# First norm of the first half: rows normalised by ScalarE, weight and bias per channel after the transpose, residual rows weighted when read back

## The chip, the core and the metric

The kernel runs on one core of a Trainium2 chip. The metric is the time of the program on the device, in microseconds (us); a row of the profile gives durations in us, means of groups in nanoseconds (ns). The core has five engines that run their own instruction queues in order: PE (TensorE, matmuls and transposes), DVE (VectorE), ACT (ScalarE), POOL (GpSimd) and SP (SyncE, which here only issues DMAs). They wait for each other by semaphores.

## The reference

One layer over 1024 positions of 1024 channels, in float32:

```python
def layer_norm(x, g, b):
    mu = jnp.mean(xf, axis=-1, keepdims=True)
    var = jnp.mean(jnp.square(xf - mu), axis=-1, keepdims=True)
    return (xf - mu) * lax.rsqrt(var + LN_EPS) * g + b
...
h = layer_norm(x, ln_in_g, ln_in_b)
u_glu, z, xbc, dt_raw, gate_a, gate_b = split_in(h @ w_in)
y_a = conformer_branch(u_glu, ...)
y_b = ssd_branch(z, xbc, dt_raw, ...)
mix = (sigmoid(gate_a) * y_a + sigmoid(gate_b) * y_b) @ w_o
h = layer_norm(DN_ALPHA * h + mix, ln1_g, ln1_b)
h = layer_norm(DN_ALPHA * h + conv_ffn(h, ...), ln2_g, ln2_b)
```

The normalised rows h are used twice: as input of the matmul with w_in, and as residual in the second norm.

## The kernel before

The 1024 positions are worked in two halves of 512, each of four tiles of 128 rows. For a half, `ln_in` loads the four x tiles, normalises them row by row on DVE, writes them to a scratch in DRAM (`h_scr`), and transposes them on PE into `hT`, which holds channels on the partitions. Then `mixers` does the two branches, `combine` gates and mixes them, and `out_proj` multiplies with w_o, adds the residual rows, which it reads back from `h_scr`, and normalises again. The order of the program is ln_in(0), mixers(0), combine(0), ln_in(1), out_proj(0), mixers(1), combine(1), and then the feed-forward part over all rows.

Precision is kept by splitting each float32 operand into a high part (a rounding cast, on ACT) and a low part (the difference, on DVE); each product is then three matmuls (L166, L167, L168). `weights` (L149) does this for a weight tile: DMA into `st_...` (L152), cast on ACT (L154), difference (L155), which is DVE's unless an engine is passed. `transpose_to` (L187) does it for four transposed blocks of 128x128 that fill one bank of PSUM: transposes on PE (L192), cast by ACT (L198), difference by DVE (L199).

The norm of a row tile is `ln_stats` (statistics L207 and L221 on DVE, square root L222 on ACT, reciprocal L223 on DVE) and `ln_apply`: two passes of DVE over 128x1024, (x - mean) * weight (L227) and times the reciprocal deviation plus bias (L230). Weight and bias are rows broadcast to all 128 partitions (`in_g`, `in_b`; `row`, L203).

`first_columns` (L348) starts on the first three column tiles of w_in before all rows are there: 144 matmuls of 128x256 (L357), where the left half (q = 0) needs the first two row tiles. For the first half (hh = 0) the low parts of these three weight tiles are made by POOL.

`out_proj` (L665) works in two column halves q of 512. For each it has four banks of PSUM, one for each row tile, and 96 matmuls; then DVE adds alpha times the residual row to each bank (L687). There are four banks of this kind, so PE begins q = 1 in a bank when L687 of q = 0 has read it.

Instructions are ordered by the tile framework: each engine's queue is fixed when the program is built, by readiness in the framework's own accounting and by priority (`tc.high_priority`). At run time each engine takes its queue in that order.

## Time and profile before

| quantity | value |
|---|---|
| median of 3 runs | 2032.83 us (2030.95 to 2035.71) |
| profiled execution, its own time | 2035.35 us |
| its span, first to last instruction | 2033.6 us |
| mean granted clock of TensorE | 0.991 |
| DMA over the span | 273.51 MB, 134 GB/s |

The time of an execution is a little longer than the span, which runs from the first to the last instruction that the profiler recorded. A row of the timeline gives the start, the duration, the engine, the line of the kernel file, the operation, its output and inputs, and in brackets how long its engine idled before and for whom. In a row of grouped instructions, the numbers behind the count are busy time in us, mean ns of one, and idle time before with its releasers.

### The profile page before, as it was taken

The page shows a single profiled execution, that of the slowest core. Times are in us where ns is not written, and L with a number is a line of the kernel's source. Part 1 is how long each engine was busy: PE and PEld are TensorE (multiplying, and loading weights), DVE is VectorE, ACT ScalarE, POOL GpSimd, SP SyncE. Part 2 cuts the span into 40 slices and gives each one's busy share as a digit, 9 for nine tenths or more (in the row PEclk, how much of TensorE's full clock was granted, in tenths as well). Part 3 has the DMA queues.
Part 4 walks back from the last instruction along what each step waited for, and adds up shares of the span by engine and source line. Part 5 has one row for each costly group of instructions (what it writes and reads, how often), then busy time and mean ns, then how long its engine had stood idle before and what let it go on. Part 6 is the DMA issues. An engine that isn't in the chain of part 4 may idle for free.

```text
span 2033.6 us, 24571 instructions
## 1 busy us (share of the span) xinstructions
PE 1978.0 (97%) x9164; PEld 1628.0 (80%) x9164; DVE 1710.7 (84%) x2285; ACT 1001.8 (49%) x1448; POOL 171.9 (8%) x141
## 2 busy tenths in 40 slices
PE   6999999999999999999999999998899999989998
PEld 6888887888788888888888888887778888777886
DVE  7599999989766869999998976596998788777868
ACT  4465654556453356665454645364334445443432
POOL 2010101001400000100100130010000000010000
PEclk9999999999999999999999999999999999999999
DMA  6212233332546522222423354565342232377563
GB/s 219 93 63 94 79 102 106 99 104 101 174 133 216 195 88 77 88 85 75 127 86 107 109 166 138 188 234 202 130 153 106 99 109 99 109 258 264 175 224 109
DMA packets 97303, 273.51 MB, mean 134 GB/s; under 512 B 11168, under 2 KB 11168, under 8 KB 97184
## 3 DMA queue, kind: packets, MB, share of 16 engines
q1 hardware_dynamic: 87696, 242.06, 35.9%
q0 software_dynamic: 7184, 25.69, 3.3%
q10 hardware_dynamic: 2304, 4.20, 0.6%
q8 instruction: 72, 1.18, 0.2%
q14 instruction: 47, 0.39, 0.1%
HBM read 222.36 MB, written 49.55 MB: 134 GB/s over the span
## 4 chain that ended last, share of the span: by engine, by line
PE 66%; DVE 24%; DMA 4%; issue 4%; ACT 1%; SPq 0%; DVEq 0%; ACTq 0%
PE acc L166 17%; PE acc L168 17%; PE acc L167 17%; DVE c L420 8%; PE sm L166 3%; PE sm L167 3%; PE sm L168 3%; DVE xbc L375 2%; DMA dr<-b_scr 1%; PE acc L357 1%; PE sm L534 1%; DVE fo L895 1%; DMA st_wo<-wo 1%; PE sm L515 1%; DVE w_so L155 1%
## 5 line engine op out<-in xcount | busy, mean ns | idle before, releaser
L420 DVE SCALAR_TENSOR_TENSOR c<-v,pc,c 128x512 f32<-128x512 f32 x480 | 375.3, 805 | 7.6 <-ACT c L409 6.1
L478 POOL TENSOR_TENSOR au<-seg_mv,head_of 128x1024 fp32r<-128x1024 f32 x32 | 76.3, 2383 | 962.2 <-PE sm L487 730.4
L166 PE MATMUL acc<-hT,w_c 128*128 128x512 f32 x352 | 141.1, 401 | 0.0
L167 PE MATMUL acc<-hT,w_c 128*128 128x512 f32 x352 | 140.7, 400 | 0.0
L168 PE MATMUL acc<-hT,w_c 128*128 128x512 f32 x352 | 138.5, 393 | 0.0
L895 DVE SCALAR_TENSOR_TENSOR fo<-u,pc,fo 128x1024 f32<-128x1024 f32 x88 | 111.5, 1279 | 8.5 <-ACT fo L891 7.8
L375 DVE SCALAR_TENSOR_TENSOR xbc<-u,pc,xbc 128x512 f32<-128x512 f32 x144 | 109.7, 774 | 0.7 <-ACT xbc L373 0.5
L167 PE MATMUL acc<-w_z,hT 128*128 128x512 f32 x256 | 100.9, 394 | 0.0
L166 PE MATMUL acc<-w_z,hT 128*128 128x512 f32 x256 | 100.9, 401 | 0.0
L168 PE MATMUL acc<-w_z,hT 128*128 128x512 f32 x256 | 100.7, 396 | 0.0
L1021 ACT CAST w_dn<-dr 128x1024 fp32r<-128x1024 f32 (+1 forms) x73 | 60.8, 842 | 77.7 <-DVE dr L951 31.5
L154 ACT CAST w_c<-st_c 128x1024 fp32r<-128x1024 f32 x50 | 52.5, 1051 | 86.8 <-PE acc L168 66.1
L1022 DVE TENSOR_TENSOR w_dn<-dr,w_dn 128x1024 fp32r<-128x1024 f32 (+1 forms) x73 | 69.6, 963 | 17.6 <-ACT w_dn L1021 17.5
L167 PEld LDWEIGHTS acc<-hT,w_c 128*128 128x128 f32 x352 | 66.2, 188 | 16.8 <-issue 3.8
L168 PEld LDWEIGHTS acc<-hT,w_c 128*128 128x128 f32 x352 | 66.1, 188 | 16.0 <-issue 2.6
L166 PEld LDWEIGHTS acc<-hT,w_c 128*128 128x128 f32 x352 | 66.1, 188 | 15.9 <-issue 2.6
L155 DVE TENSOR_TENSOR w_c<-st_c,w_c 128x1024 fp32r<-128x1024 f32 x47 | 60.6, 1289 | 20.2 <-ACT w_c L154 20.2
L166 PE MATMUL acc<-h1s,w_s 128*128 128x512 f32 x168 | 66.6, 397 | 5.7 <-ACT u L875 5.7
L166 PE MATMUL acc<-h1b,w_ue 128*128 128x512 f32 x176 | 68.9, 392 | 2.6 <-ACT w_ue L740 1.4
L166 PE MATMUL sm<-h1b,w_s 128*128 128x512 f32 x176 | 70.3, 400 | 0.0
L167 PE MATMUL sm<-h1b,w_s 128*128 128x512 f32 x176 | 70.3, 399 | 0.0
L168 PE MATMUL sm<-h1b,w_s 128*128 128x512 f32 x176 | 69.9, 397 | 0.0
(352 smaller groups left out, 5811.1 us busy)
## 6 DMA issues: line engine op xcount, KB each, us to landing
st_c<-wcol SPq DMA_DIRECT2D x50, 512.0 KB, 3.5
st_z<-wz SPq DMA_DIRECT2D x32, 512.0 KB, 3.4
st_wo<-wo SPq DMA_DIRECT2D x24, 512.0 KB, 3.8
ra<-wup SPq DMA_DIRECT2D x22, 512.0 KB, 3.6
rb<-wup SPq DMA_DIRECT2D x22, 512.0 KB, 3.4
t_scr<-fo POOLq DMA_DIRECT2D x22, 512.0 KB, 4.2
dr<-t_scr SPq DMA_DIRECT2D x44, 256.0 KB, 3.4
dr<-wdown SPq DMA_DIRECT2D x38, 256.0 KB, 3.8
```

The source lines that it names most:

```text
L154: A.copy(w[:, 0, :], st)
L155: (eng or V).tensor_tensor(out=w[:, 1, :], in0=st, in1=w[:, 0, :].bitcast(F32), op=ALU.subtract)
L166: TE.matmul(ps, wa(0), xa(0), start=start, stop=False, skip_group_check=more)
L167: TE.matmul(ps, wa(0), xa(1), start=False, stop=False, skip_group_check=more)
L168: TE.matmul(ps, wa(1), xa(0), start=False, stop=stop, skip_group_check=more)
L357: TE.matmul(ps[:, ts], w[:, i, k * P : (k + 1) * P], hT[:, j, k, ts], start=n == 0 and k == 0, stop=n == 2 and k == KD - 1,)
L375: V.scalar_tensor_tensor(out=o, in0=u[:, k : k + HALF], scalar=pc[:, wc + k : wc + k + 1], in1=o, op0=ALU.mult, op1=ALU.add,)
L420: V.scalar_tensor_tensor(out=accs[i], in0=v[:, k : k + HALF], scalar=pc[:, wc + k : wc + k + 1], in1=accs[i], op0=ALU.mult, op1=ALU.add,)
L478: G.tensor_tensor(out=au, in0=seg_mv[:, c, :].unsqueeze(1).to_broadcast([P, 8, P]), in1=head_of[:, g, :].unsqueeze(2).to_broadcast([P, 8, P]),
L895: V.scalar_tensor_tensor(out=o, in0=u[:, k : k + T], scalar=pc[:, wc + k : wc + k + 1], in1=o, op0=ALU.mult, op1=ALU.add,)
L1021: A.copy(w[:, 0, cs], src)
L1022: V.tensor_tensor(out=w[:, 1, cs], in0=src, in1=w[:, 0, cs].bitcast(F32), op=ALU.subtract)
```

## The change

The first half gets a norm of its own, `ln_first`. The two affine steps of the norm are taken apart. (x - mean) / deviation is one activation on ACT per row tile, with the scale 1/deviation and a shift of -mean/deviation per row. Weight and bias of the norm come after the transpose, when channels are partitions and both are one number per partition (new columns of `pc`, the per-channel constants): ACT and DVE take turns in evicting 128x128 blocks from PSUM into a float32 tile `v`, from which the high part (ACT) and the low part (DVE) are made. The rows written to `h_scr` are without weight and bias; `out_proj` of the first half loads the two broadcast rows (`res_g`, `res_b`) and applies them on POOL to the rows read back. The four loads of x are preceded by a small load of the new constants, and PE does 40 transposes of the identity at the start. The low parts of the first three weight tiles are DVE's instead of POOL's. The second half's norm is as before.

```diff
@@ -39,7 +39,9 @@
-PC_N = PC_FB + 44
+PC_IG = PC_FB + 44
+PC_IB = PC_IG + 8
+PC_N = PC_IB + 8
...
@@ -231,31 +233,73 @@
+    def ln_first():
+
+        hT = big_tile("hT0")
+        with pool("lnin0", side="right") as pl:
+            with tc.high_priority(offset=8000):
+                SY.dma_start(pc[:, PC_IG:PC_N], pcol[:, PC_IG:PC_N])
+                xts = []
+                for t in range(4):
+                    xt = pl.tile([P, D], F32, name=f"x0_{t}")
+                    SY.dma_start(xt, x[t * P : (t + 1) * P, :])
+                    xts.append(xt)
+                for n in range(10):
+                    pt = bank(1)
+                    for i in range(4):
+                        TE.transpose(pt[:, i * P : (i + 1) * P], ident, ident)
+            SY.dma_start(pc[:, :PC_IG], pcol[:, :PC_IG])
+            SY.dma_start(a_log, prow[RW_AL : RW_AL + HEADS].partition_broadcast(P))
+            SY.dma_start(dskip, prow[RW_SD : RW_SD + HEADS].partition_broadcast(P))
+            for t, xt in enumerate(xts):
+                ts = slice(t * P, (t + 1) * P)
+                with tc.high_priority(offset=6000 - 1000 * (t // 2)):
+                    mv, rs = ln_stats(pl, [xt], f"in0_{t}")
+                    shift = pl.tile([P, 1], F32, tag="shift", bufs=2, name=f"shift{t}")
+                    V.tensor_scalar(
+                        out=shift, in0=mv[:, 0, 0:1], scalar1=rs[:, 0:1], scalar2=-1.0,
+                        op0=ALU.mult, op1=ALU.mult,
+                    )
+                    A.activation(out=xt, in_=xt, func=AF.Identity, scale=rs[:, 0:1], bias=shift)
+                    SY.dma_start(h_scr[0][ts, :], xt)
+                    for q in range(2):
+                        pt = bank(0)
+                        for i in range(4):
+                            c = (4 * q + i) * P
+                            TE.transpose(pt[:, i * P : (i + 1) * P], xt[:, c : c + P], ident)
+                        v = pl.tile([P, 4, P], F32, tag="v", bufs=3, name=f"v0_{t}_{q}")
+                        for i in range(4):
+                            k = 4 * q + i
+                            src = pt[:, i * P : (i + 1) * P]
+                            g, b = pc[:, PC_IG + k : PC_IG + k + 1], pc[:, PC_IB + k : PC_IB + k + 1]
+                            if i % 2:
+                                V.tensor_scalar(
+                                    out=v[:, i, :], in0=src, scalar1=g, scalar2=b,
+                                    op0=ALU.mult, op1=ALU.add,
+                                )
+                            else:
+                                A.activation(out=v[:, i, :], in_=src, func=AF.Identity, scale=g, bias=b)
+                        hi, lo = (hT[:, i, 4 * q : 4 * q + 4, ts] for i in range(2))
+                        A.copy(hi, v)
+                        V.tensor_tensor(out=lo, in0=v, in1=hi.bitcast(F32), op=ALU.subtract)
+        return hT
+
     def ln_in(hh):
         hT = big_tile(f"hT{hh}")
         with pool(f"lnin{hh}", side="right") as pl:
-            first = hh == 0
-            xts, gb = [], []
+            gb = [row(pl, RW_ING, D, "in_g"), row(pl, RW_INB, D, "in_b")]
+            xts = []
...
@@ -347,7 +391,7 @@
-        ws = [weights(wcol[ct], f"c{hh}_{ct}", eng=None if hh else G) for ct in cts]
+        ws = [weights(wcol[ct], f"c{hh}_{ct}") for ct in cts]
...
@@ -668,6 +712,10 @@
         for t in range(4):
             SY.dma_start(rs[t], h_scr[hh][t * P : (t + 1) * P, :])
+        ing, inb = row(pl, RW_ING, D, "res_g"), row(pl, RW_INB, D, "res_b")
+        for r in rs:
+            G.tensor_tensor(out=r, in0=r, in1=ing, op=ALU.mult)
+            G.tensor_tensor(out=r, in0=r, in1=inb, op=ALU.add)
         sts = [pl.tile([P, 2, 6], F32, name=f"st_o{hh}_{t}") for t in range(4)]
...
@@ -1100,7 +1148,7 @@
-    hT = ln_in(0)
+    hT = ln_first()
```

`out_proj` is called for the first half alone; the second half has `out_proj_pairs`, which is unchanged.

The change also moves instructions. In the file of the change, all lines behind `ln_first` have other numbers: L230 becomes L232, L199 becomes L201, L155 becomes L157, L687 becomes L735.

First, ACT's queue at the very start of the program. Before, it is square roots (L222), casts of transposed blocks (L198, of PSUM banks sm) and casts of the first column weights (L154, w_c):

```order
L198 CAST hT_184<-sm_214 128x4x128
L198 CAST hT_184<-sm_221 128x4x128
L154 CAST w_c_40_306<-st_c_40_304 128x1024
L198 CAST hT_184<-sm_239 128x4x128
L154 CAST w_c_32_311<-st_c_32_309 128x1024
L198 CAST hT_184<-sm_246 128x4x128
L222 ACTIVATE rs_in_2_254<-mv_in_2_253,eps 128x1
L154 CAST w_c_36_316<-st_c_36_314 128x1024
L222 ACTIVATE rs_in_3_279<-mv_in_3_278,eps 128x1
L198 CAST hT_184<-sm_264 128x4x128
```

Now, the normalising activations (L263), block evictions (L281, into v) and casts of v (L283) stand in it. The rows up to the cast of v_1_0 are what the first column matmuls need:

```order
L263 ACTIVATE x_0_189<-x_0_189,shift_258,rs_in_0_251 128x1024
L281 ACTIVATE v_0_0_267<-sm_262,pc 128x128
L156 CAST w_c_40_397<-st_c_40_395 128x1024
L263 ACTIVATE x_1_191<-x_1_191,shift_294,rs_in_1_287 128x1024
L224 ACTIVATE rs_in_2_323<-mv_in_2_322,eps 128x1
L281 ACTIVATE v_0_1_279<-sm_274,pc 128x128
L281 ACTIVATE v_0_0_267<-sm_262,pc 128x128
L156 CAST w_c_32_402<-st_c_32_400 128x1024
L224 ACTIVATE rs_in_3_359<-mv_in_3_358,eps 128x1
L156 CAST w_c_36_407<-st_c_36_405 128x1024
L281 ACTIVATE v_1_0_303<-sm_298,pc 128x128
L263 ACTIVATE x_2_193<-x_2_193,shift_330,rs_in_2_323 128x1024
```

The evictions of different banks alternate in the queue, and the weight casts stand between them; six more rows (the norm of x_3 among them) follow before the cast of v_1_0.

Second, DVE's queue around the residual addition of the first half, where ln_in(1) is under way. Before:

```order
L227 SCALAR_TENSOR_TENSOR x_3_5153<-x_3_5153,mv_in_3_5234,in_g 128x1024
L223 RECIPROCAL rs_in_2_5210<-rs_in_2_5210 128x1
L687 SCALAR_TENSOR_TENSOR r_0_5263<-r_0_5263,acc_5279 128x512
L687 SCALAR_TENSOR_TENSOR r_1_5264<-r_1_5264,acc_5280 128x512
L687 SCALAR_TENSOR_TENSOR r_2_5265<-r_2_5265,acc_5281 128x512
L199 TENSOR_TENSOR hT_5143<-sm_5170,hT_5143 128x4x128
L223 RECIPROCAL rs_in_3_5235<-rs_in_3_5235 128x1
L199 TENSOR_TENSOR hT_5143<-sm_5177,hT_5143 128x4x128
L687 SCALAR_TENSOR_TENSOR r_3_5266<-r_3_5266,acc_5282 128x512
L230 SCALAR_TENSOR_TENSOR x_2_5151<-x_2_5151,rs_in_2_5210,in_b 128x1024
```

Now, from the second pass over x_2 on:

```order
L232 SCALAR_TENSOR_TENSOR x_2_5246<-x_2_5246,rs_in_2_5301,in_b 128x1024
L201 TENSOR_TENSOR hT_5234<-sm_5261,hT_5234 128x4x128
L201 TENSOR_TENSOR hT_5234<-sm_5268,hT_5234 128x4x128
L201 TENSOR_TENSOR hT_5234<-sm_5286,hT_5234 128x4x128
L232 SCALAR_TENSOR_TENSOR x_3_5248<-x_3_5248,rs_in_3_5326,in_b 128x1024
L201 TENSOR_TENSOR hT_5234<-sm_5293,hT_5234 128x4x128
L201 TENSOR_TENSOR hT_5234<-sm_5311,hT_5234 128x4x128
L157 TENSOR_TENSOR w_wo_1_2_5574<-st_wo_1_2_5572,w_wo_1_2_5574 128x1024
L201 TENSOR_TENSOR hT_5234<-sm_5318,hT_5234 128x4x128
L201 TENSOR_TENSOR hT_5234<-sm_5336,hT_5234 128x4x128
L201 TENSOR_TENSOR hT_5234<-sm_5343,hT_5234 128x4x128
L735 SCALAR_TENSOR_TENSOR r_0_5354<-r_0_5354,acc_5382 128x512
```

The addition to r_0 (L687, now L735) stood ahead of the second pass over x_2 and x_3 and of the low parts of hT; it now stands behind all of them and behind the split of w_wo_1_2.

Third, the new rows of POOL, behind the last row of the first half's conv norm (r_0 to r_3 are the residual tiles of the first half):

```order
L682 TENSOR_TENSOR var_4876<-var_4876,csq_7_4904 128x512
L717 TENSOR_TENSOR r_0_5354<-r_0_5354,res_g 128x1024
L717 TENSOR_TENSOR r_1_5355<-r_1_5355,res_g 128x1024
L717 TENSOR_TENSOR r_2_5356<-r_2_5356,res_g 128x1024
L717 TENSOR_TENSOR r_3_5357<-r_3_5357,res_g 128x1024
L718 TENSOR_TENSOR r_0_5354<-r_0_5354,res_b 128x1024
L718 TENSOR_TENSOR r_1_5355<-r_1_5355,res_b 128x1024
```

Where POOL had nothing between the end of the first half's conv norm and the second half's scan, it has eight passes (the additions to r_2 and r_3 are not shown); all multiplications stand ahead of the additions. On SP the two loads of `res_g` and `res_b` stand behind the four row loads, `res_g` ahead of the load of w_wo_1_2 and `res_b` ahead of that of w_wo_1_3. On PE, all 16 transposes of x_2 and x_3 in ln_in(1) now stand ahead of the first matmul of q = 1; before, they stood among these matmuls.

More of the change, by code (lines that the diff above doesn't have):

```diff
@@ L244, in ln_in @@
                     xts.append(xt)
[L245 to L258 removed]
+            for t, xt in enumerate(xts):
+                mv, rs = ln_stats(pl, [xt], f"in{hh}_{t}")
+                ln_apply(xt, mv, rs, 0, *gb)
+                SY.dma_start(h_scr[hh][t * P : (t + 1) * P, :], xt)
+                transpose_to(hT, xt, t, 0, KD)
         return hT
@@ L1179, in _pack @@
             chan(a["ffn_dw_b"][0]).T,
+            chan(a["ln_in_g"]).T,
+            chan(a["ln_in_b"]).T,
         ],
```

13 lines of the change are left out of this document (removed).

## The prediction

> **What bounds the kernel now.** I read the page first (busy shares and the chain of work that ended last), then the waits of PE, then the timeline of the two places that the change touches.
>
> ```profile
> PE 1978.0 (97%) x9164; PEld 1628.0 (80%) x9164; DVE 1710.7 (84%) x2285; ACT 1001.8 (49%) x1448; POOL 171.9 (8%) x141
> PE 66%; DVE 24%; DMA 4%; issue 4%; ACT 1%; SPq 0%; DVEq 0%; ACTq 0%
> PE sm L192 <- DVE x L230: 15.4, 3, 12.7
> ```
>
> PE is busy 97% of the span, and the chain runs through PE for 66%. POOL is all but idle. The longest wait of PE in the whole trace is for the normalised rows of L230, 15.4 us in three pieces, 12.7 of it at the start, which is what this change rewrites. The rest of the kernel is a nearly gapless queue on PE, so a delay of PE early on goes through unless something later has slack. Two places matter: the first 40 us (first half's norm) and 647 to 689 us, where the rows are read back as residual.
>
> **Place one, the front.** Rows of the timeline and of two tiles (x count, then min/median/max ns):
>
> ```profile
> 4.33 1.29 DVE L207 BATCH_NORM_STATS2 st_in<-x 128x6 f32<-128x512 f32 x2 [1.73 <-DMA x<-x]
> 8.83 2.48 DVE L227 SCALAR_TENSOR_TENSOR x<-x,mv_in,in_g 128x1024 f32<-128x1024 f32 x2 [1.58 <-DMA in_g<-prow]
> 12.71 3.40 PE L192 MATMUL sm<-ident,x 128*128 128x128 f32 x16 [12.71 <-DVE x L230]
> 17.99 5.12 DVE L227 SCALAR_TENSOR_TENSOR x<-x,mv_in,in_g 128x1024 f32<-128x1024 f32 x2
> 26.59 1.06 PE L192 MATMUL sm<-ident,x 128*128 128x128 f32 x8 [1.60 <-DVE x L230]
> L155 POOL TENSOR_TENSOR w_c<-st_c,w_c x3: 2395/3363/3375, 16.3 to 22.0; 128x1024 fp32r<-128x1024 f32 x3
> 29.95 9.36 PE L357 MATMUL acc<-hT,w_c 128*128 128x256 f32 x74
> 39.61 0.50 PE L166 MATMUL acc<-hT,w_c 128*128 128x512 f32 x1
> 689.23 17.43 PE L357 MATMUL acc<-hT,w_c 128*128 128x256 f32 x144
> L891 ACT ACTIVATE fo<-u,pc 128x1024 f32<-128x1024 f32 x44 | 49.7, 1149 | 20.1 <-DVE fo L923 8.7 <-DMA t_scr<-fo 5.2 <-DMA b_scr<-fo 4.1
> L154 ACT CAST w_c<-st_c 128x1024 fp32r<-128x1024 f32 x50 | 52.5, 1051 | 86.8 <-PE acc L168 66.1 <-issue 8.6 <-PE acc L357 6.8
> L373 ACT ACTIVATE xbc<-acc,pc 128x512 f32<-128x512 f32 x48 | 33.1, 689 | 0.0
> L371 ACT COPY u<-acc 128x512 f32<-128x512 f32 x48 | 27.6, 575 | 0.0
> L511 ACT COPY bt<-sm 128x128 f32<-128x128 f32 x28 | 7.3, 262 | 27.1 <-DVE cbm L498 27.1
> L182 ACT CAST mixT<-mb 128x512 fp32r<-128x512 f32 x16 | 10.0, 623 | 5.7 <-DVE mb L661 5.7
> 708.28 0.56 ACT L371 COPY u<-acc 128x512 f32<-128x512 f32 x1
> 708.74 0.19 ACT L372 COPY u<-u_halo 128x3 f32<-128x3 f32 x1
> L222 ACT ACTIVATE rs_in<-mv_in,eps 128x1 f32<-128x1 f32 x8 | 2.4, 299 | 12.4 <-DVE mv_in L221 8.8 <-DVE x L230 3.6
> ```
>
> What goes: the wait for in_g (1.58 us), four DVE pairs of 1024-wide passes, and the three POOL splits, whose contention stretched two of those passes to 5.12 us. What comes: one more small load ahead of x (estimate half a microsecond, so x_0 at 4.8), 40 warm-up transposes on PE while it has nothing else, and a chain on ACT. DVE's statistics of x_0 and x_1 (1.29 each, with the aggregates and the reciprocal between) let the first normalising activation start at about 8.0. ACT works in order, and up to the cast that gives the first column matmuls their last 128 columns (v_1_0) it has: 4 norms at 1.15 (nearest row L891, same shape) = 4.60; 3 casts of w_c at 1.05 = 3.15; 3 casts into hT at 0.62 (L182) = 1.87; 7 block evictions; 2 square roots at 0.30 = 0.60. A 128x128 eviction with scale and bias does not occur; L373 against L371 says that scale and bias add 0.114 to a plain copy, L511 that a plain 128x128 copy takes 0.262, so 0.38 each (0.26 to 0.45) = 2.66. Sum 12.9. An ACT start can lie before the end of the one ahead (by 0.10 at 708.74); 0.07 for 18 of them is -1.3; the evictions alternate between ACT and DVE on one PSUM bank, for which I add 1.0: columns begin at 8.0 + 12.9 - 1.3 + 1.0 = 20.6. DVE's share (blocks, and now the three lo splits of w_c at about 1.2) runs beside it. Then 144 column matmuls: half 1 shows 17.43 for the same 144 without a gap; four transposes that stand among them add 0.5, handing over 0.4: first 512-wide matmul at 38.9, against 39.61, **-0.7**.
>
> The clock decides the sign. The 16 transposes at 12.71 took 0.213 each, the eight at 26.59 0.133, so PE starts slow. The warm-up ends near 8 us; then come 28 transposes in pieces between 11 and 20 with PE mostly idle. If PE is slow again at 20.6, its first microseconds cost 1.6 (bounds below), so **+0.9**. The row for that comes from the other place. The Trainium skill ("TensorE: Matmul & The Clock Gate", What's actually happening) says that the throttle is the default and returns after an idle window of about 3.4 us; the idle PE between 8 and 11 would by that rule undo the warm-up, which gives the same +0.9. I take +0.9; ends -1.3 (evictions at 0.32, PE fast) and +2.5 (transposes slow too, on ACT's path).
>
> **Place two, the residual.** Rows of the timeline, of SyncE's DMA queue and of PE around it, of L670, and two stretches (PE, PEld, DVE, ACT, POOL busy, granted clock, DMA share, GB/s):
>
> ```profile
> DMA to landing us min/median/max: 10.8/10.9/11.0
> L670 SPq DMA_DIRECT2D r<-h_scr x4: 319/323/327, 647.3 to 650.9; - x4
> 653.03 1.56 SPq L152 DMA_DIRECT2D st_wo<-wo  x2
> SPq L152 <- DMA in_g<-prow: 1.7, 1, 1.7
> 656.00:658.00 2.00, 2.00 (x11) 1.65 (x10) 2.00 (x3) 0.00 (x0) 0.00 (x0) 1.00 1.03 420
> 655.03 0.39 PE L166 MATMUL acc<-w_wo,mixT 128*128 128x512 f32 x1
> 655.71 0.39 PE L166 MATMUL acc<-w_wo,mixT 128*128 128x512 f32 x1
> 663.09 1.86 DVE L687 SCALAR_TENSOR_TENSOR r<-r,acc 128x512 f32<-128x512 f32 x3
> 663.90 0.47 PE L166 MATMUL acc<-w_wo,mixT 128*128 128x512 f32 x1 [0.85 <-DVE r L687]
> 667.58 0.44 PE L166 MATMUL acc<-w_wo,mixT 128*128 128x512 f32 x1
> 664.00:668.00 4.00, 4.00 (x11) 3.15 (x12) 4.00 (x8) 0.67 (x1) 0.00 (x0) 0.57 0.61 249
> 666.72 1.28 DVE L230 SCALAR_TENSOR_TENSOR x<-x,rs_in,in_b 128x1024 f32<-128x1024 f32 x1
> L199 DVE TENSOR_TENSOR hT<-sm,hT 128x512 fp32r<-128x512 f32 x16 | 10.5, 677 | 2.7 <-ACT hT L198 2.7
> 670.90 1.21 DVE L155 TENSOR_TENSOR w_wo<-st_wo,w_wo 128x1024 fp32r<-128x1024 f32 x1
> 704.94 1.23 DVE L155 TENSOR_TENSOR w_c<-st_c,w_c 128x1024 fp32r<-128x1024 f32 x1 [1.34 <-ACT w_c L154]
> ```
>
> Before: PE cannot begin the second column half (q=1) until L687 frees a bank of q=0, at 663.90. It then stands 25.3 us off the first column of half 1 (689.23): 96 matmuls at 0.227 (655.03 to 655.71 is three) = 21.8, 16 transposes about 1.9, and 1.6 of slow clock (nine matmuls from 663.90 to 667.58 take 3.68 instead of 2.04; the clock was 0.57 there after a short pause of PE).
>
> After, ahead of L687 (L735 in the changed file) stand POOL's passes over r: four multiplications by res_g, then the first addition of res_b, because the order has all multiplications first. res_g is issued where the wo load is now, 653.0 (it waits for the same in_g). The row transfers ahead of it take 10.8 us to land since the DMA engines are full at 420 GB/s; r_3, issued at 650.9, lands at 661.7, and 0.5 MB more at 420 GB/s is 1.25: res_g at **663.0**. A POOL pass of this size with two SBUF operands took 2395 ns undisturbed and 3363 beside DVE passes with two SBUF operands. Three such DVE passes stand in the stretch (L230 of x_2 and of x_3, and the split of w_wo_1_2), so 5 x 2.395 + 3 x 0.97 = 14.9, and r_0 is ready at **677.9**. With L687 (0.68) and the handing over (663.09 to 663.90 less 0.68: 0.13) PE restarts at **678.7**. The additions for r_1 to r_3 come 2.4 us apart, faster than PE's 24 matmuls (5.4 us) to a bank, so no second wait. All 16 transposes that were among the q=1 work now stand ahead of it and fall into the wait; half 1 starts at 678.7 + 21.8 + 1.6 = 702.1, **+12.9**.
>
> Bounds: all five passes undisturbed, restart 675.7, +9.9; all five at 3363, 680.6, +14.8; res_g later by 1.5 (the res_b and wo loads share the transfers), +14.4. A rule bears on this: the Trainium skill ("SBUF — State Buffer", two separate sides) calls the port pair of GpSimd and VectorE an exclusive lock, held for a whole instruction. The rows agree (0.97 us more, less than one DVE pass of 1.2 to 1.3); by the strict rule the three meetings cost up to 1.28 each and the term would be +13.8.
>
> Loading 1 MB more here and 1 MB less in the front costs nothing by itself: the front's transfers are not what PE waits for after 20 us. POOL's last three additions end 7 us after r_0 and nothing else waits for POOL then. The removed loads of in_g and in_b in the front are hidden likewise.
>
> **Sum.** +0.9 and +12.9 = +13.8 on the profiled execution (span 2033.6, its time 2035.35). The median of the three runs shown is 2032.83, so 2046.6.
>
> **Rivals.**
> 1. POOL undisturbed (the lock seldom met): +9.9 + 0.9 = 2043.6. For it: DVE waits for transposes between its passes; against: 3363 and 3375 are two of the three POOL passes that exist beside DVE work.
> 2. DVE's order sets the restart, not POOL. In the changed order L687 stands behind all eight L199, both late L230 and the split: 2 x 1.2 + 8 x 0.6 + 1.13 + two reciprocals 0.1 = 8.5 us of pieces at their start-to-start distance that were behind it. From 663.09 it would come at 671.6; PE restarts at 672.4, and with the transposes out of q=1, half 1 starts at 695.8: +6.6, in all 2040.3. It decides if POOL takes under 8.6 us for its five passes; 2395 speaks against it.
> 3. Not slower: the delay is swallowed in half 1. In the chain of work PE hands over to DVE at 900 (by way of a cast):
>
> ```profile
> 899.92 1.06 ACT w_z L154
> 902.75 1.41 DVE xbc L375 x2
> ```
>
> If DVE's queue sets the end from there and could work ahead while PE waits, nothing of place two is left: 2032.83 + 0.9 = 2033.7, or 2030 with a good front. It decides if DVE, after 689, had work whose inputs are ready earlier. The row at 704.94 speaks against: DVE itself idles there 1.34 us for a cast that follows PE's columns, so it is late as PE is.
> 4. The front gains more than the residual costs: needs the first 512-wide matmul before 27, which 12.9 us of work on ACT from 8.0 and 17.4 on PE exclude.
> 5. Worse: res_g late and every pass contended, the front at its upper end: +14.8 + 1.5 + 2.5 = 2051.6; beyond that only if PE's wait makes a weight load collide later.
>
> **How the numbers follow.** Forecast, POOL's chain sets the restart with some contention: 0.62; rival 1: 0.13; rival 2: 0.07; rival 3: 0.07 (0.05 of it within 0.2%, 0.02 faster); rival 4: 0.01; worse, rival 5: 0.10. About 0.2%, 4 us, is what a measurement of this kernel can tell from no change. Faster 0.03, same 0.05, slower 0.92. Predicted 2046.6; the range 2038 to 2052 leaves out the not-slower cases and half of rival 5.
>
> **What would show it.** Place one: the first L269 transposes of x near 10, the first column matmul near 20.6, the first 512-wide matmul at 38 to 42. Place two: res_g landing at 663, POOL L717 and L718 passes of 2.4 to 3.4 from there, the first L735 near 678, a wait of PE of some 13 to 15 us for r, and the columns of half 1 from 702. Right in sum but wrong in step: L735 behind DVE work rather than POOL (rival 2). Wrong altogether: columns of half 1 late by 13 but the end late by less than 5 (rival 3); the difference of the two traces' times at L357 of half 1 and at the end shows it.

## The result and the profile after

| kernel | median | runs | change in us |
|---|---|---|---|
| before | 2033.96 us | 2030.95 to 2035.71 (4) | |
| after | 2057.87 us | 2052.78 to 2058.22 (4) | +23.9 |

The ratio is 1.011, with a 95% interval of 1.0089 to 1.013. The change makes the kernel slower, and by 10 us more than was forecast (+13.8); 2057.87 lies above the range of 2038 to 2052.

The profiled execution after took 2058.17 us, with a span of 2056.5 us. The page's busy shares and its chain of work:

```profile
PE 1996.1 (97%) x9204; PEld 1637.2 (80%) x9204; DVE 1710.1 (83%) x2300; ACT 1012.8 (49%) x1468; POOL 183.3 (9%) x146
PE 78%; DVE 13%; DMA 4%; issue 3%; ACT 1%; POOL 1%; SPq 0%; DVEq 0%; ACTq 0%; POOLq 0%
```

PE's busy time has grown by 18 us (1978.0 before). The 40 transposes of the identity, which are new, take 6.9 of them (first row below). In the other 11 us work of the same size takes PE longer, which is not a wait; spells of a slow clock in the two places are a part of it. That is the first hint that something else than these two places may be slower.

**Place one.** The timeline of the front (start, duration, engine, line, operation):

```profile
1.67 6.93 PE L250 MATMUL acc<-ident 128*128 128x128 f32 x40 [1.67 <-POOL ident masks.py:199]
8.69 1.22 ACT L263 ACTIVATE x<-x,shift,rs_in 128x1024 f32<-128x1024 f32 x1
9.97 1.09 PE L269 MATMUL sm<-ident,x 128*128 128x128 f32 x8 [1.37 <-ACT x L263]
13.25 1.92 PE L269 MATMUL sm<-ident,x 128*128 128x128 f32 x8 [2.19 <-ACT x L263]
13.28 0.79 ACT L281 ACTIVATE v<-sm,pc 128x128 f32<-128x128 f32 x2
21.40 2.65 PE L401 MATMUL acc<-hT,w_c 128*128 128x256 f32 x12
24.24 16.07 PE L401 MATMUL acc<-hT,w_c 128*128 128x256 f32 x132
40.61 0.51 PE L168 MATMUL acc<-hT,w_c 128*128 128x512 f32 x1
```

The window view shows the clock. A row has the stretch and its length, the busy time of PE, its weight loads, DVE, ACT and POOL with counts in brackets, then the granted clock, the DMA share and GB/s:

```profile
8.00:13.00 5.00, 1.69 (x14) 1.22 (x12) 4.57 (x14) 3.76 (x5) 0.00 (x0) 1.00 1.00 383
18.00:23.00 5.00, 4.18 (x19) 3.49 (x18) 4.00 (x9) 4.88 (x11) 0.00 (x0) 0.50 0.94 332
23.00:28.00 5.00, 5.00 (x42) 5.00 (x41) 4.60 (x11) 4.62 (x12) 0.00 (x0) 0.94 0.36 138
```

The columns begin at 21.40 (20.6 was forecast), the first 512-wide matmul stands at 40.61, 1.0 us later than before (39.61; +0.9 was forecast). The eight transposes from 9.97 take 1.09, those from 13.25 take 1.92: PE's clock has dropped in between, as assumed, and it is still at 0.50 when the columns begin. From 21.40 to 40.61 are 19.2 us. Half 1 takes 17.3 for the same 144 matmuls (702.36 to 719.63), and the transposes among and behind the columns take 0.7, which leaves 1.2 for the slow clock. By this reckoning the first 512-wide matmul would have stood at about 39.4 without it, ahead of the 39.61 before: the clock did decide the sign.

**Place two.** Waits of PE over the whole span, then rows of POOL, DVE and PE:

```profile
PE acc L168 <- DVE r L735: 8.9, 1, 8.9
663.96 11.73 POOL L717 TENSOR_TENSOR r<-r,res_g 128x1024 f32<-128x1024 f32 x4 [106.39 <-ACT hT L200]
675.65 9.34 POOL L718 TENSOR_TENSOR r<-r,res_b 128x1024 f32<-128x1024 f32 x4
669.01 2.18 DVE L157 TENSOR_TENSOR w_wo<-st_wo,w_wo 128x1024 fp32r<-128x1024 f32 x1
678.02 0.69 DVE L735 SCALAR_TENSOR_TENSOR r<-r,acc 128x512 f32<-128x512 f32 x1 [5.04 <-POOL r L718]
678.85 0.77 PE L168 MATMUL acc<-w_wo,mixT 128*128 128x512 f32 x1 [8.88 <-DVE r L735]
702.36 17.44 PE L401 MATMUL acc<-hT,w_c 128*128 128x256 f32 x144
```

POOL starts at 663.96, its four multiplications take 11.73 (2.93 each) and its additions 2.34 each; DVE is idle for 5.04 us waiting for the first sum, and PE restarts at 678.85, where 678.7 was forecast. The columns of half 1 begin at 702.36 (702.1 was forecast), 13.1 us late against 689.23. DVE paid as well: the split of w_wo_1_2 took 2.18 beside POOL, where 1.21 was usual.

**The rest.** Half 1 begins within 0.3 us of the forecast, but the span ends 22.9 us late. The further loss is found with one landmark, the first matmul of the feed-forward part that meets the rows h1s, and windows that count PE's instructions. Before:

```profile
1405.84 0.79 PE L166 MATMUL sm<-h1s,w_s 128*128 128x512 f32 x1 [5.30 <-ACT w_s L740]
1900.00:2000.00 100.00, 100.00 (x443) 82.86 (x442) 70.87 (x95) 45.48 (x61) 0.00 (x0) 1.00 0.59 188
```

After:

```profile
1421.47 0.79 PE L168 MATMUL sm<-h1s,w_s 128*128 128x512 f32 x1 [5.33 <-ACT w_s L788]
1550.00:1750.00 200.00, 200.00 (x868) 162.33 (x867) 163.75 (x187) 93.29 (x112) 11.22 (x21) 1.00 0.29 102
1900.00:2000.00 100.00, 100.00 (x439) 82.05 (x438) 76.59 (x100) 42.02 (x53) 0.00 (x0) 1.00 0.63 204
```

At the landmark the changed kernel is 15.6 us late, at the end 22.9: 2.5 us came in between 702 and 1421, and 7.3 in the 630 us behind it. In the window from 1900 PE is busy without a gap and at full clock in both kernels, and yet does 443 matmuls before and 439 after. Single rows show it as the distance from start to start, which is 0.227 before:

```profile
1901.53 0.39 PE L168 MATMUL acc<-w_dn 128*128 128x512 f32 x1
1901.75 0.39 PE L169 MATMUL acc<-w_dn 128*128 128x512 f32 x1
1901.98 0.40 PE L170 MATMUL acc<-w_dn 128*128 128x512 f32 x1
1902.22 0.40 PE L168 MATMUL acc<-w_dn 128*128 128x512 f32 x1
1902.45 0.39 PE L169 MATMUL acc<-w_dn 128*128 128x512 f32 x1
```

The steps here are 0.22, 0.23, 0.24 and 0.23. Such a slow spell comes back every 24 matmuls, that is with every second weight tile: a tile serves 12 matmuls, and the code takes the w_dn tiles in turn from the two ends of SBUF. The diff has one thing that can reach so far: the constants `pc` are 16 columns, 64 bytes a partition, wider. `pc` is allocated as `const.tile([P, PC_N + 80], ...)`, of which the last 80 columns are never used, and all tiles allocated behind it from the same end of SBUF should now lie 64 bytes higher (the traces show no addresses). Tiles allocated from the other end (`side="right"`, among them h1s and some of the w_dn) stay where they were.

### The profile page after: what moved, and what is told of

It is laid out like the page before. It is cut to its first block, busy times and chain, and to the rows that moved or that the text cites. A ratio compares the mean times of both kernels' runs of the same rounds, so it can differ in the third digit from the quotient of the medians.

```text
span 2056.5 us, 24708 instructions
## 1 busy us (share of the span) xinstructions
PE 1996.1 (97%) x9204; PEld 1637.2 (80%) x9204; DVE 1710.1 (83%) x2300; ACT 1012.8 (49%) x1468; POOL 183.3 (9%) x146
## 4 chain that ended last, share of the span: by engine, by line
PE 78%; DVE 13%; DMA 4%; issue 3%; ACT 1%; POOL 1%; SPq 0%; DVEq 0%; ACTq 0%; POOLq 0%
PE acc L168 19%; PE acc L169 19%; PE acc L170 19%; DVE c L464 6%; PE sm L168 4%; PE sm L169 4%; PE sm L170 4%; PE acc L401 2%; PE sm L578 2%; DMA dr<-b_scr 1%; PE sm L559 1%; PE sm L567 1%; DVE w_so L157 1%; DVE xbc L419 1%; DMA ln_g<-prow 1%
## 5 line engine op out<-in xcount | busy, mean ns | idle before, releaser
L157 DVE TENSOR_TENSOR w_c<-st_c,w_c 128x1024 fp32r<-128x1024 f32 x50 | 64.2, 1283 | 25.2 <-ACT w_c L156 25.1
```

What stands on the lines that cost most here:

```text
L157: (eng or V).tensor_tensor(out=w[:, 1, :], in0=st, in1=w[:, 0, :].bitcast(F32), op=ALU.subtract)
```

## The experiments

Each was timed beside runs of the kernel before on the same chip. The ratios are to those, with 95% intervals.

| run | what | median | before | ratio |
|---|---|---|---|---|
| e1_pad_restored | after, 64 bytes less padding | 2050.47 | 2033.43 | 1.0085 (1.007 to 1.01) |
| e2_before_shifted | before, 64 bytes more padding | 2037.79 | 2033.43 | 1.0026 (1.0016 to 1.0036) |
| e3_residual_alone | before with place two's part | 2051.43 | 2033.43 | 1.0091 (1.0077 to 1.0105) |
| e4_front_alone | after without it, padding restored | 2036.21 | 2033.43 | 1.0012 (1.0003 to 1.0021) |
| e5_shift128 | before, 128 bytes more | 2036.67 | 2033.66 | 1.0017 (1.0008 to 1.0026) |
| e6_shift256 | before, 256 bytes more | 2033.72 | 2033.66 | 1.0001 (0.9992 to 1.0009) |
| e7_u_width | before, three tiles 128 bytes wider | 2032.03 | 2033.66 | 0.9989 (0.998 to 0.9998) |
| e8_pool_in_front | after, POOL's passes in the front | 2042.84 | 2033.66 | 1.0046 (1.0033 to 1.0058) |
| e9_row_by_row | after, POOL row by row | 2047.26 | 2034.63 | 1.0071 (1.0057 to 1.0085) |
| e10_front_kept_warm | front alone, PE kept busy | 2035.5 | 2034.63 | 1.0007 (0.9998 to 1.0016) |
| e11_front_repaired | after with e10's front, e8's passes held back, the padding, e7's width | 2041.86 | 2034.63 | 1.0041 (1.0027 to 1.0054) |
| e12_both_ends_64 | before, both ends' tiles 64 bytes on | 2033.51 | 2034.27 | 0.9997 (0.9988 to 1.0006) |

### Is it the 64 bytes?

```diff
# e1, on the kernel after
-    pc = const.tile([P, PC_N + 80], F32, name="pc")
+    pc = const.tile([P, PC_N + 64], F32, name="pc")
# e2, on the kernel before
-    pc = const.tile([P, PC_N + 80], F32, name="pc")
+    pc = const.tile([P, PC_N + 96], F32, name="pc")
```

> The changed kernel with 16 columns less of unused padding behind the per-channel constants (PC_N + 64 for PC_N + 80), so that every tile behind them in SBUF lies where it lay before the change; the queues of PE, DVE and ACT are the same as in the changed kernel. Theory A (64 bytes of address cost PE about 1% in the feed-forward part): PE's pitch there goes back from about 231 ns to 228 ns and below, the time falls by 6 to 8 us, to about 2050. Rival (the slower pitch is a state of the chip, or comes from the wait of PE and its clock): 2056 to 2058, no change against the changed kernel.

> The kernel before with 16 more columns of unused padding (PC_N + 96), which shifts every tile behind it by 64 bytes as the change does, and nothing else. Theory A: slower by 6 to 8 us, about 2040 to 2042, all of it from 1400 us on. Rival: within 2 us of the kernel before.

e1 brought 2050.47, so the distance to the kernel before falls from 23.9 to 17.0 us: by the medians the 64 bytes cost 6.9. With four runs each, the intervals of these two ratios touch (1.0089 to 1.013 and 1.007 to 1.01); the counts of matmuls carry more here. e2, which does nothing but shift, loses 4.4 us. The window view of e1 and then of e2:

```profile
1550.00:1750.00 200.00, 200.00 (x876) 164.15 (x876) 162.89 (x186) 92.50 (x111) 11.23 (x21) 1.00 0.29 103
1900.00:2000.00 100.00, 100.00 (x443) 82.81 (x442) 75.16 (x98) 43.70 (x55) 0.00 (x0) 1.00 0.63 203
```

```profile
1550.00:1750.00 200.00, 198.62 (x860) 160.77 (x859) 157.16 (x180) 92.20 (x112) 10.67 (x20) 1.00 0.28 99
1900.00:2000.00 100.00, 100.00 (x439) 82.01 (x438) 69.83 (x93) 44.92 (x62) 0.00 (x0) 1.00 0.59 190
```

The count goes back to 443 where the padding is restored (and from 868 to 876 in the window from 1550, which has no gap in either kernel), and falls to the 439 of the changed kernel where only the padding is shifted. The rival (a state of the chip, or an effect of PE's waits) is out: e2 has none of the waits, and its instructions stand in the order of the kernel before. Theory A was too high for e2's time (6 to 8 us expected, 4.4 measured). The loss of pace alone comes to 6.8 us there (table below); e2's profile has shorter spells of slow clock than that of the kernel before (mean clock 0.995 against 0.991), which may hide the difference. That is argued, not shown.

```diff
# e5 and e6, on the kernel before
-    pc = const.tile([P, PC_N + 80], F32, name="pc")
+    pc = const.tile([P, PC_N + 112], F32, name="pc")   # e5
+    pc = const.tile([P, PC_N + 144], F32, name="pc")   # e6
# e7, on the kernel before
-    us = [upp.tile([P, T + 32], F32, name=f"u{i}") for i in range(3)]
+    us = [upp.tile([P, T + 64], F32, name=f"u{i}") for i in range(3)]
```

> The kernel before with 32 more padding columns (PC_N + 112): the tiles behind the per-channel constants lie 128 bytes higher, against the tiles at the other end of SBUF, which do not move. Theory (PE is slower when the moving operand and the weights of a matmul lie at different offsets within 256 bytes): slow as with 64 bytes, PE drifts by some 5 us between 1400 us and the end, time 2036 to 2040. Rival (the period is 128 bytes or less): no drift, within 2 us of the kernel before.

> The kernel before with 64 more padding columns (PC_N + 144): 256 bytes higher. Theory (only the offset within 256 bytes counts): no drift, within 2 us of the kernel before. Rival (the place itself counts, or the distance to other tiles): a drift of several us.

> The kernel before with the three tiles u of up_rest 32 columns wider (T + 64 for T + 32), so that a tile is 17 x 256 bytes and the weights behind it lie at the same offset within 256 bytes as the rows they meet. Theory: the matmuls of L166 to L168 with sm<-h1b,w_s, half of which have a pitch of 233 ns in the kernel before, fall to 227 ns, some 260 matmuls by 6 ns: 1.5 to 2 us faster. Rival: no change.

All three came as the theory said. A shift of 128 bytes costs 3.0 us, one of 256 bytes nothing (1.0001), and the wider u gains 1.6 us. The same stretch of 200 us in the up stage, kernel before, then e5, e6 and e7:

```profile
1550.00:1750.00 200.00, 198.60 (x870) 162.70 (x869) 159.25 (x182) 92.10 (x113) 10.68 (x20) 1.00 0.28 99
```

```profile
1550.00:1750.00 200.00, 198.61 (x860) 161.12 (x860) 157.21 (x180) 89.90 (x109) 10.67 (x20) 1.00 0.28 99
```

```profile
1550.00:1750.00 200.00, 198.60 (x869) 162.70 (x868) 159.30 (x181) 92.43 (x112) 10.67 (x20) 1.00 0.29 101
```

```profile
1550.00:1750.00 200.00, 198.59 (x874) 163.62 (x874) 160.59 (x184) 92.58 (x112) 11.21 (x21) 1.00 0.29 101
```

PE's gaps are the same in all four (1.4 us), the counts are 870, 860, 869 and 874. So it is the offset within 256 bytes that counts: e6 moved the tiles farthest and lost nothing. In the kernel before one group of weights in the up stage already lies 128 bytes off the rows that it meets; e7 puts that right and is the one kernel here that is faster than both. Its gain is small, 0.11% with an interval that ends just below 1.

These runs do not yet say whether a tile's own place counts, or its place against another tile's. The last one moves both ends of SBUF by the same 64 bytes:

```diff
# e12, on the kernel before
+    padp = ctx.enter_context(pool("padr", side="right"))
+    pad = padp.tile([P, 48], F32, name="padr")
+    V.memset(pad, 0.0)
     state_stack = ExitStack()
...
-    pc = const.tile([P, PC_N + 80], F32, name="pc")
+    pc = const.tile([P, PC_N + 96], F32, name="pc")
```

> The kernel before with 64 bytes more of padding behind pc (as e2) and a pad of 192 bytes a partition ahead of all tiles of the other end, which moves those down by 192, that is up by 64 within 256. Every tile now stands 64 bytes further within 256 bytes than in the kernel before, and no tile against another (one memset of 128x48 on VectorE is added, at the start, a fraction of a microsecond). Theory A (what counts is the offset of one tile against another): 2032 to 2035 us, ratio 0.9995 to 1.0006, and 443 matmuls in the window from 1900 to 2000, about 870 from 1550 to 1750. Rival (what counts is where a tile stands by itself within 256 bytes, for PE's reads or for the DMAs that write it): as e2 or worse, 2037 to 2041 us, ratio 1.002 to 1.004, with 439 and about 860 matmuls.

```profile
1550.00:1750.00 200.00, 198.60 (x869) 162.59 (x868) 159.19 (x182) 92.54 (x112) 10.68 (x20) 1.00 0.29 100
1900.00:2000.00 100.00, 100.00 (x443) 82.84 (x442) 70.82 (x96) 44.97 (x61) 0.00 (x0) 1.00 0.58 187
```

The left tiles stand exactly where e2 has them, and yet the counts are those of the kernel before, and so is the time (0.9997). What counts is the offset of one tile against another, as theory A said; the rival is out.

The traces also say which matmuls it is. The table has the mean distance in ns from the start of one 512-wide matmul to the next; distances from 300 ns up, which are gaps and the slow clock, are left out. The last row multiplies the changes of pace of all such groups by their counts:

| matmuls | before | e2 | e5 | e6 | e12 | e7 | after | e1 |
|---|---|---|---|---|---|---|---|---|
| acc<-h1s,w_s (rows from one end, weights from the other) | 228.1 | 233.4 | 232.9 | 228.0 | 228.2 | 227.2 | 233.3 | 228.0 |
| sm<-h1b,w_s (both from the end of pc) | 230.3 | 230.6 | 230.7 | 230.2 | 230.4 | 226.9 | 230.5 | 230.5 |
| acc<-w_dn (both operands in one tile, tiles in turn from both ends) | 226.9 | 229.1 | 228.0 | 226.8 | 226.9 | 226.8 | 229.2 | 226.8 |
| all, us against before (after: against e1) | | +6.8 | +5.9 | -0.2 | +0.2 | -2.7 | +7.0 | |

The ends are those of the code. The pair whose operands stand at opposite ends slows with the shift, and the pair that shares an end does not; e7, which moves tiles of one end against each other, speeds up that one. The pace explains the 6.9 us between e1 and the changed kernel. What stays open is the mechanism: in the down stage both operands of a matmul lie in one tile, and it is slower too when the tiles taken in turn with it lie at another offset. No run told these apart.

### Is place two POOL's chain, and what does each part cost alone?

```diff
# e3, on the kernel before: out_proj as in the change
+        ing, inb = row(pl, RW_ING, D, "res_g"), row(pl, RW_INB, D, "res_b")
+        for r in rs:
+            G.tensor_tensor(out=r, in0=r, in1=ing, op=ALU.mult)
+            G.tensor_tensor(out=r, in0=r, in1=inb, op=ALU.add)
# e4, on the kernel after: PC_N + 64, and these four lines taken out
```

> The kernel before with the residual part of the change alone: the two row loads and the eight POOL passes in out_proj. The weight and bias of the norm are applied twice to the residual rows. Theory (POOL's five passes hold L687, and what PE loses there goes through to the end): PE restarts near 679, the first columns of half 1 start 12 us late, the end is 12 to 14 us late, 2046 to 2048. Rival (part of the delay of the changed kernel comes from its front): under 8 us late.

> The changed kernel with the padding restored and without the residual part: the residual rows of the first half go without weight and bias of the first norm. Theory: the front alone costs 1.0 to 1.4 us (first 512-wide matmul at 40.6), place two is as before, the time 2033 to 2036, not to be told from the kernel before. Rival (the front's reordering costs or gains later): more than 4 us away from it.

e3 is 18.0 us slower, e4 2.8 us. Of e3, whose first 512-wide matmul stands at 38.71, 0.9 us ahead of the kernel before:

```profile
662.79 12.23 POOL L673 TENSOR_TENSOR r<-r,res_g 128x1024 f32<-128x1024 f32 x4 [107.42 <-ACT hT L198]
678.18 0.77 PE L166 MATMUL acc<-w_wo,mixT 128*128 128x512 f32 x1 [6.57 <-DVE r L691]
701.93 17.44 PE L357 MATMUL acc<-hT,w_c 128*128 128x256 f32 x144
```

With the old front, POOL's chain is the same and the columns of half 1 come 12.7 us late: place two needs nothing of the front. Counted from its own front it costs 13.6. The end is later still (15.6 us in the spans, 18.0 in the medians): 2.7 us came in between 1316 and the landmark, 1.8 of them a wait of PE for residual rows in out_proj of the second half. The changed kernel and e1 wait 0.5 and 0.6 there, the kernel before and e9 not at all. The expectation (12 to 14) was too low; what the 2.4 us between spans and medians are, no trace shows.

In the medians e4 and e3 add up to 20.8 us, against 17.0 of e1, but each has an interval of 2 to 3 us to both sides. In the spans of the profiled executions they do add up: 1.5 + 15.6 against 17.5. Two rows of e4:

```profile
41.84 0.50 PE L168 MATMUL acc<-hT,w_c 128*128 128x512 f32 x1
687.44 17.43 PE L401 MATMUL acc<-hT,w_c 128*128 128x256 f32 x144
```

The front alone is 2.2 us late at the first and 1.8 us early at the second (39.61 and 689.23 before), so 645.6 us lie between the two, where the kernel before has 649.6. The new code also moves work within ln_in(1), and PE begins q = 1 without a pause. How much of the 4.0 us is due to that is open: e2 and e12, in the order of the kernel before and with its pause, have 648.5 and 646.7, and the clock stayed at 1.00 from 664 to 668 there, where it was 0.57 in the profiled execution before. The gain is gone by the landmark (1406.42 against 1405.84), and in the changed kernel, where PE has to wait for POOL, it does not arise.

```diff
# e9, on the kernel after with PC_N + 64
+        ing, inb = row(pl, RW_ING, D, "res_g"), row(pl, RW_INB, D, "res_b")
         for t in range(4):
             SY.dma_start(rs[t], h_scr[hh][t * P : (t + 1) * P, :])
-        ing, inb = row(pl, RW_ING, D, "res_g"), row(pl, RW_INB, D, "res_b")
-        for r in rs:
-            G.tensor_tensor(out=r, in0=r, in1=ing, op=ALU.mult)
-            G.tensor_tensor(out=r, in0=r, in1=inb, op=ALU.add)
+        for t, r in enumerate(rs):
+            with tc.high_priority(offset=100 * (4 - t)):
+                G.tensor_tensor(out=r, in0=r, in1=ing, op=ALU.mult)
+                G.tensor_tensor(out=r, in0=r, in1=inb, op=ALU.add)
```

> The changed kernel with the padding restored, the two row loads res_g and res_b issued ahead of the residual rows, and POOL's passes row by row, so that r_0 needs three passes instead of five. Theory (POOL's passes ahead of r_0 set PE's restart): r_0 ready near 670, then DVE's queue (its work ahead of the addition to r_0 ends at 673) is what is late; PE restarts at 673 to 674 instead of 678.8 and the time is 4 to 6 us below that with the padding alone (2050.5): 2044.5 to 2046.5. Rival (DVE's order or the loads set the restart anyway): no change, 2050.

Rows of e9:

```profile
669.65 3.34 POOL L719 TENSOR_TENSOR r<-r,res_b 128x1024 f32<-128x1024 f32 x1
674.60 0.67 DVE L736 SCALAR_TENSOR_TENSOR r<-r,acc 128x512 f32<-128x512 f32 x1
675.42 0.76 PE L168 MATMUL acc<-w_wo,mixT 128*128 128x512 f32 x1 [2.56 <-DVE r L736]
699.60 17.43 PE L401 MATMUL acc<-hT,w_c 128*128 128x256 f32 x144
```

Two POOL passes fewer ahead of r_0, and PE restarts at 675.42, half 1 at 699.60 (e1: 704.26). DVE does not idle ahead of the addition any more: as expected, its own queue is now what is late. The time fell by 3.2 us against e1, or by 4.4 if each is counted from the kernel before as timed beside it; 4 to 6 were expected. The intervals of the two ratios overlap, so the rows carry this more than the times. The restart is 1.4 us behind the expected 673 to 674: POOL's three passes up to r_0 take 9.8 us, 3.3 each, and DVE's passes beside them are stretched too (3.30 us for the one over x_2 at 664.16).

### Can the change be mended?

```diff
# e8, on the kernel after with PC_N + 64 and without the four lines in out_proj
-                    SY.dma_start(h_scr[0][ts, :], xt)
...
+            ing, inb = row(pl, RW_ING, D, "in_g"), row(pl, RW_INB, D, "in_b")
+            for t, xt in enumerate(xts):
+                G.tensor_tensor(out=xt, in0=xt, in1=ing, op=ALU.mult)
+                G.tensor_tensor(out=xt, in0=xt, in1=inb, op=ALU.add)
+                SY.dma_start(h_scr[0][t * P : (t + 1) * P, :], xt)
```

> The changed kernel with the padding restored, and with the eight POOL passes moved from out_proj to the front: POOL multiplies and adds on the rows of x after they are transposed, and h_scr gets the finished rows. Theory (the cost of the residual part is its place ahead of L687, not POOL's work): the 12.6 us of place two go, the time is that of the front alone, 2034 to 2037. Rival (POOL's passes in the front hold DVE's low parts by the shared use of SBUF, or the loads of the two rows hold weights): columns late by 5 us and more.

The rival was right: 9.2 us slower. The columns begin at 21.74, but they are held on the way, and the first 512-wide matmul stands at 46.58, 4.7 us behind e4's. The low parts of hT on DVE (tile view: count, then min/median/max ns), of e4 and then of e8:

```profile
L284 DVE TENSOR_TENSOR hT<-v,hT x8: 680/689/695, 18.4 to 27.9; 128x512 fp32r<-128x512 f32 x8
```

```profile
L283 DVE TENSOR_TENSOR hT<-v,hT x8: 1340/2526/2875, 18.3 to 37.3; 128x512 fp32r<-128x512 f32 x8
```

A pass of 0.69 us on DVE takes 2.53 in the median beside POOL passes of 2.8. These passes have two operands in SBUF, since the change takes them from v and not from PSUM.

```diff
# e10, on the kernel of e4: behind each bank of transposes of x_0 to x_2
+                        if t < 3:
+                            for n in range(2):
+                                pf = bank(1)
+                                for i in range(4):
+                                    TE.transpose(pf[:, i * P : (i + 1) * P], ident, ident)
# e11: the front of e10, u of e7, no store of xt to h_scr ahead of this, and the end of ln_first
+            G.tensor_copy(ing[:, 0:1], hT[:, 1, KD - 1, HALF - 1 : HALF].bitcast(F32))
+            SY.dma_start(ing, prow[RW_ING : RW_ING + D].partition_broadcast(P))
+            SY.dma_start(inb, prow[RW_INB : RW_INB + D].partition_broadcast(P))
+            for t, xt in enumerate(xts):
+                G.tensor_tensor(out=xt, in0=xt, in1=ing, op=ALU.mult)
+                G.tensor_tensor(out=xt, in0=xt, in1=inb, op=ALU.add)
+                SY.dma_start(h_scr[0][t * P : (t + 1) * P, :], xt)
```

> The front alone (padding restored, residual rows without weight and bias of the first norm), with 48 more transposes of the identity on PE between the transposes of x, so that PE does not stand idle between 8.6 and 21 us. Theory (the slow clock from 13 to 26 us makes the front late): the clock stays full, the transposes of x take 1.1 us for eight instead of 2.0, the first 512-wide matmul is at 38.5 to 39.5 instead of 40.6 to 42.0, the time 2 to 3 us below the front alone (2036.2). Rival (ACT's chain alone sets the front): under 1 us.

> All that the runs point to, with the reference's result: the front of the change kept warm as in e10_front_kept_warm, POOL's eight passes in the front but held back until the last low part of hT is done (a one-element copy of it into the tile of the weight row makes the row's load wait), the padding restored, u 32 columns wider. Theory: POOL then meets no pass that PE waits for, so the time is that of e10_front_kept_warm less 1.7 us: 2031 to 2033, the level of the kernel before with the wider u alone. Rival (POOL meets the first convolutions' passes on DVE instead): 3 us and more above.

e10 did not bring what was expected. Its rows:

```profile
13.39 1.09 PE L269 MATMUL sm<-ident,x 128*128 128x128 f32 x8
18.28 1.09 PE L269 MATMUL sm<-ident,x 128*128 128x128 f32 x8 [2.05 <-DVE v L281]
22.59 2.61 PE L406 MATMUL acc<-hT,w_c 128*128 128x256 f32 x12
41.74 0.50 PE L168 MATMUL acc<-hT,w_c 128*128 128x512 f32 x1
```

The transposes are fast now (1.09), but the columns begin at 22.59, 1.3 us later than in e4 (21.25). PE waits 2.05 and 2.45 us for banks that the evictions free, and ACT's queue has another order: it idles 1.93 us for a weight load ahead of a cast at 11.14 and evicts its first block at 13.43, where e4 evicts one at 10.52. During these waits the granted clock fell after all, from 1.00 until 20 us to 0.50 from 22 to 24, so the first 12 columns are as slow as in the changed kernel (2.61 against 2.65). From the start of the columns to the first 512-wide matmul e10 takes 19.2 us and e4, whose clock stays at 0.50 until 26, 20.6: about as much is won there as is lost before. So e10 shows that ACT's queue and the banks bound the start of the columns; it is no test of a front whose clock stays full. The time, 0.7 us below the front alone, cannot be told from it. e11 missed its 2031 to 2033 too, at 2041.86: POOL meets the splits of the next weights on DVE instead, four of which took 2.22 to 3.38 us beside POOL's 22.9 us of passes, where 1.23 is usual. That these splits are what the end is late by was not tested. So the change was not mended by any of these; the kernel before with the wider u (e7) stays the fastest.

## Why the prediction was right in its two places and wrong in its sum

- **Place one** was right in time, in part by luck: +0.9 forecast, +1.0 in the profile of the changed kernel, and between +1.8 and +2.4 in later runs with this front. The columns began 0.8 us later than worked out, since the chain on ACT started at 8.69 rather than 8.0 (the chain itself took 12.7 us, forecast 12.6), and from there to the first 512-wide matmul it took 0.7 us less than worked out: 19.2 for 19.9. The two errors cancel. The reason for the sign was right: the slow clock cost 1.2 us where 1.6 was taken, and in e4, where it lasted until 26 us, the same stretch took 1.4 us more, which is why e4's front is later. As the prediction has it, the idle PE behind the warm-up undid it: the clock fell near 13.4 us, behind two idle stretches of 1.37 and 2.19 us.
- **Place two** was right in mechanism; its times agree so closely by luck. POOL started at 663.96 (663.0 forecast) and took 14.1 us to the first sum (14.9), so that PE's restart at 678.85 (678.7) has two errors that cancel. Half 1 at 702.36 (702.1) includes the front's delay, which the forecast adds to it; counted from its own front, place two cost 12.1 and not 12.9. PE's wait for r is 8.9 us and not 13 to 15, since the transposes that moved ahead of q = 1 fill the rest with waits of 2.19 and 0.84 between them. e3 shows the mechanism without the new front, e9 shows that it is the count of passes ahead of r_0. Rival 2 was the next limit: DVE's own work ended at 672.98 in the changed kernel (671.6 worked out), and in e9, with two passes fewer, DVE's queue sets the restart, later than worked out because POOL stretches its passes.
- **POOL beside DVE**: the rows agree with the rule cited from the Trainium skill ("SBUF — State Buffer", two separate sides), and more strictly than the forecast used it: in e8 a DVE pass of 0.69 takes 2.53, nearly the length of a whole POOL pass. The forecast counted only what POOL loses; DVE loses too (2.18 for 1.21 in the changed kernel).
- **Not swallowed** (rival 3): right. Half 1 begins 13.1 us late and the first matmul with w_wo of its q = 0 stands at 1318.39, where it stood at 1303.31: 15.1 us. A wait of DVE near 990 us added 1.6: an activation there waited 4.57 us for its buffer's write to DRAM, 2.98 before. Of PE's time it shows as waits for the state, 2.6 us in all (1.7 before); over all traces these lie between 0.5 and 2.7, so what of them is due to the change is not known.
- **The step that failed** is the sum: it has two terms, and takes the pace of PE behind 702 us as unchanged without a reason. The prediction says that the small load of new constants costs half a microsecond ahead of x and speaks nowhere of the tile that it goes into. The tile grew by 64 bytes, with the unused 80 columns left as they were, and from then on every tile behind it lay 64 bytes off the tiles of the other end. The runs put 4.4 us (e2) to 6.9 us (e1 against the changed kernel) on this, the pace of PE's matmuls 7.0. With the padding restored the same change takes 2050.47, against 2046.6 forecast and inside the range of 2038 to 2052. In e1's profile the 17.5 us are 2.4 for the front (0.9 forecast), 12.6 for place two (12.9), 1.4 between 702 and the landmark and 1.1 behind it.
- The danger could be seen beforehand, though not its price: the unused columns behind `pc` stand in the quoted kernel, and a tile that grows moves what comes after it. In the trace of before, matmuls of one shape have two paces in the up stage (those of h1b with w_s have 230.3 ns in the mean, of w_dn 226.9), and e7 takes that away.

The Trainium skill ("SBUF — State Buffer", 🔬 SBUF: two separate sides) says that on the engines' side only the port pair of GpSimd and VectorE causes contention and that PE never waits for anyone there. The measured pace of PE differs by 0.9% over a stretch without gaps at full clock (876 matmuls in e1, 868 in the changed kernel) by nothing but where tiles lie. Whether that is contention or PE's own reading, the runs do not say.

## What to carry to other kernels

A diff that changes the size of an early, long-lived tile changes the place of everything allocated behind it: before timing the edit itself, give the tile back its old size in bytes with padding, or time the padding alone. Work handed to an idle engine is not free if its result has a consumer in a queue: count the passes ahead of the first consumer, not the total, and see what it shares with the engine beside it. Count PE's instructions in a gapless window of the same work in both traces, at the same granted clock: if the numbers differ, no wait explains the loss. If a forecast is met, look at its terms: here both places met theirs by errors that cancel.

## What the runs showed of the hardware

- PE's pace depends on the offset of tiles against each other within 256 bytes: shifting one end's tiles by 64 or 128 bytes costs 4.4 and 3.0 us of 2033, shifting them by 256 bytes or both ends by 64 costs nothing, and lining up one group that was 128 bytes off gains 1.6 us. A matmul with rows at one end and weights at the other takes 233.4 instead of 228.1 ns at 64 bytes off.
- A 128x512 pass of DVE with two operands in SBUF took 2.53 us in the median instead of 0.69 beside POOL's passes of 2.8 us.
- Idle transposes can hold PE's clock: in e10 48 of them kept it at 1.00 until 20 us (eight transposes in 1.09 us instead of 1.92 to 1.97). It fell to 0.50 behind two waits of 2.05 and 2.45 us with only eight transposes between them.
